# Neighbourhood attention block: sums of the output weights made in memory by accumulating transfers, another order of the last step's products, and the bias laid out in memory

## The chip, the core and the metric

The kernel runs on one core of a Trainium2 chip. The metric is device microseconds of one execution; the kernel before takes 899.82 us, the median of 3 runs (899.55 to 900.76). Engines are called as in the profile: PE multiplies matrices, PEld loads its weights, DVE and ACT work element by element, POOL and SP issue transfers (POOL also computes a few small values), and each engine works off its instructions in order. A profile of one execution shows every instruction with its times.

## The reference

One layer of an encoder over 512 tokens (an 8 x 64 grid) of width 2048, all in float32. The weights are two matrices, 2048 x 8192 in and 2048 x 2048 out.

```python
h = rms_norm(x, norm_pre)
q, k, v, z = jnp.split(h @ na_w_in, 4, axis=-1)          # 16 heads of 128
# each token attends to 8 rows x 16 columns of keys around its own column
s = einsum('bqhd,bxqyhd->bhqxy', q_r, k_nb) * scale + rpb[:, dr, dc]
o = einsum('bhqxy,bxqyhd->bqhd', softmax(s), v_nb)
y = (o * silu(z)) @ na_w_out
out = x + rms_norm(y, norm_post)
```

## The kernel before

Work goes in ten steps. Steps 0 to 7 multiply the input by the columns of the in-weights that two heads need (512 columns a step, the q, k, v and z of one pair of heads); steps 8 and 9 multiply the gated attention by the out-weights, 1024 columns in each. Steps 0 and 8 are plain products (32 k-steps, each 12 matmuls). Steps 1 to 7 and 9 use Strassen's scheme in Winograd's form: seven passes of eight k-steps, 6 matmuls in a k-step, over sums of blocks of the input (A11, S1, A12, N2, A22, N4, N3, made once) and sums of blocks of the weights (made as they come). Every float32 operand is split into `hi` (rounded, by ACT) and `lo` (the rest, by DVE), and a product is three matmuls: hi x hi, the input's lo x hi, hi x lo. A k-step is called m, and `base(step)` is a step's first; `k` below is the k-step inside a pass.

`prep(m)` makes `hi` and `lo` of the weights of k-step m, two k-steps (`AHEAD`) before the products; three buffers of each exist. The weights come from two places. `T[k]`, eight buffers, holds the running sum of weight blocks: pass 0 takes it as loaded, passes 1, 3 and 4 add a block to it on DVE (L234), pass 5 adds another for pass 6 (L249). `raw`, four buffers (`NRAW`), takes the blocks that are added or used as they are; SP issues a raw's load as soon as the buffer is free, that is when DVE has used the raw of four k-steps of that kind before.

In the last step (step 9, `LAST`) the passes run in the order `LATE`, pass 2 last, so that its result, which only the first two row blocks need, comes in two halves. `chain(p)` names the accumulator of a pass: X for 0 and 2, Y for 1, 3 and 5, Z for 4 and 6. `combine` reads the accumulators after a pass and keeps `c["12"]`, `c["21"]`, `c["22"]`. The 512 rows of the result are four blocks t; blocks 0 and 1 come from pass 5 (columns n = 3) and pass 2 (n = 2), blocks 2 and 3 from pass 6. `finish(n, t, ...)` squares a piece on ACT and scales it by `gpost` on DVE; when all four pieces of a block have their squares, POOL computes `rcy`, and `final(t)` adds each piece to the residual `xres` (four updates on DVE) and stores it. `load_res` loads the residuals on SP: in the last step, those of blocks 2 and 3 at one per k-step from pass 1 on.

Work beside the products (the attention of the heads, residuals, ends) is hung on k-steps by `at(m, f)`. What is issued through `sync`, `dve`, `act` (class `InOrder`) keeps the order in which it is written; all else may be moved by the scheduler, so the order on an engine is not the order of the code.

The relative bias of a head is loaded by `load_bias` (POOL's queue) as 128 overlapping rows `braw`, and `bias` adds the mask to a reversed view of it on DVE, three operations a head, into `bm`, which `add_bias` adds to the scores. A head's gated result goes to memory (`graw`, POOL's queue) and comes back in step 8. The squares of x for the first norm are loaded (`sq`) during step 0.

## Time and profile before

| | us |
|---|---|
| median of 3 runs | 899.82 |
| the profiled execution | 903.68 |
| its span | 901.9 |
| PE busy | 880.9 |
| DVE busy | 755.3 |
| ACT busy | 561.2 |
| POOL busy | 29.7 |
| span from the last matmul's end (889.34) | 12.6 |

The span is the time from the first to the last record of the profiled execution; the execution's own time is 1.8 us longer. A profile's times are compared with each other, and the medians with each other. In a timeline row stand start, length, engine, line, operation, output<-inputs, and in brackets how long the engine had been idle and what ended that. A row of the stretches gives for each engine its busy time and the number of its instructions.

### The profile page before, as it was taken

Reading aid. Unit: us, or ns where it says so; the run is one execution under the profiler, and the core shown is the slowest. Engines: PE = TensorE matmul, PEld = TensorE weight load, DVE = VectorE, ACT = ScalarE, POOL = GpSimd, SP = SyncE. Lnnn points to the kernel's source line nnn. Section 1 sums busy time; section 2 is a strip of 40 time slices with the busy share of each in tenths; the row PEclk is TensorE's granted clock in tenths of the full one; section 3 lists DMA queues with packets and bytes.
Section 4 is the critical chain, followed back from the end, with each engine's and each line's share of the span. In section 5 each row is a group of like instructions: output and inputs, shape, how many; then the busy total and the mean of one; then the engine's idle time right before and its main releaser. Section 6 shows DMA issues by size and latency. Waiting matters only on the chain. (4 is left out here: it accounts for less than half of the span.)

```text
span 901.9 us, 13169 instructions
## 1 busy us (share of the span) xinstructions
PE 880.9 (98%) x4184; PEld 731.3 (81%) x4184; DVE 755.3 (84%) x1415; ACT 561.2 (62%) x1089; POOL 29.7 (3%) x59
## 2 busy tenths in 40 slices
...
GB/s 256 237 258 131 105 138 210 217 130 162 219 214 111 190 227 192 95 218 210 176 112 219 210 176 110 239 200 149 137 278 205 157 93 119 158 122 254 245 179 186
DMA packets 85878, 163.32 MB, mean 181 GB/s; under 512 B 10017, under 2 KB 10017, under 8 KB 85809
## 3 DMA queue, kind: packets, MB, share of 16 engines
...
q8 instruction: 32, 0.52, 0.2%
q10 hardware_dynamic: 432, 0.53, 0.2%
...
## 5 line engine op out<-in xcount | busy, mean ns | idle before, releaser
L241 ACT CAST hi<-t 128x512 fp32r<-128x512 f32 x320 | 196.8, 618 | 137.3 <-DVE lo L242 31.1
L242 DVE TENSOR_TENSOR lo<-t,hi 128x512 fp32r<-128x512 f32 x320 | 218.1, 687 | 25.8 <-ACT hi L241 24.9
L242 DVE TENSOR_TENSOR lo<-raw,hi 128x512 fp32r<-128x512 f32 x184 | 125.8, 689 | 62.8 <-ACT hi L241 50.3
L241 ACT CAST hi<-raw 128x512 fp32r<-128x512 f32 x184 | 113.6, 620 | 98.9 <-PE u L279 18.7
L234 DVE TENSOR_TENSOR t<-t,raw 128x512 f32<-128x512 f32 x192 | 128.5, 688 | 13.0 <-DMA raw<-in_w 12.5
L279 PE MATMUL u<-hi,a 128*128 128x512 f32 x512 | 133.1, 397 | 3.4 <-ACT hi L241 2.1
L279 PEld LDWEIGHTS u<-hi,a 128*128 128x128 f32 x512 | 96.2, 191 | 24.3 <-ACT hi L241 2.6
L279 PE MATMUL u<-lo,a 128*128 128x512 f32 x256 | 70.8, 390 | 0.0
L279 PEld LDWEIGHTS u<-lo,a 128*128 128x128 f32 x256 | 48.2, 188 | 10.1
L249 DVE TENSOR_TENSOR t<-t,raw 128x512 f32<-128x512 f32 x64 | 42.8, 688 | 1.2 <-DMA raw<-in_w 1.1
L149 DVE TENSOR_TENSOR a<-x,a 128x256 fp32r<-128x256 f32 (+1 forms) x24 | 11.6, 512 | 19.5 <-ACT a L148 19.5
L450 DVE TENSOR_TENSOR bm<-braw,mask_sb 128x256 f32<-128x256 f32 x48 | 27.4, 601 | 0.0
L322 PE MATMUL u1Y<-hi,a 128*128 128x512 f32 x96 | 26.8, 396 | 0.0
L322 PE MATMUL u6Y<-hi,a 128*128 128x512 f32 x96 | 26.8, 396 | 0.0
L322 PE MATMUL u5Y<-hi,a 128*128 128x512 f32 x96 | 26.8, 396 | 0.0
L322 PE MATMUL u7Y<-hi,a 128*128 128x512 f32 x96 | 26.8, 396 | 0.0
L322 PE MATMUL u3Y<-hi,a 128*128 128x512 f32 x96 | 26.8, 396 | 0.0
L322 PE MATMUL u4Y<-hi,a 128*128 128x512 f32 x96 | 26.8, 396 | 0.0
L322 PE MATMUL u2Y<-hi,a 128*128 128x512 f32 x96 | 26.8, 396 | 0.0
L322 PE MATMUL u9Y<-hi,a 128*128 128x512 f32 x96 | 26.6, 392 | 0.0
L444 POOL DMA_DIRECT2D braw<-in_rpb x16 | 8.5, 534 | 437.9 <-DVE bm L450 253.5
L322 PEld LDWEIGHTS u9Y<-hi,a 128*128 128x128 f32 x96 | 17.9, 188 | 4.3 <-ACT s L341 0.4
(444 smaller groups left out, 1953.2 us busy)
## 6 DMA issues: line engine op xcount, KB each, us to landing
raw<-in_w SPq DMA_DIRECT2D x384, 256.0 KB, 3.0
t<-in_w SPq DMA_DIRECT2D x128, 256.0 KB, 3.0
x<-in_xT SPq DMA_DIRECT2D x16, 256.0 KB, 4.4
xres<-in_x SPq DMA_DIRECT2D x16, 256.0 KB, 6.2
graw<-zm POOLq DMA_DIRECT2D x14, 256.0 KB, 3.7
out<-xres SPq DMA_DIRECT2D x14, 256.0 KB, 3.2
...
braw<-in_rpb POOLq DMA_DIRECT2D x16, 184.0 KB, 3.6
```

Source lines behind the costliest of these rows:

```text
L149: (vector or nc.vector).tensor_tensor(lo, src, hi.bitcast(F32), ALU.subtract)
L234: nc.vector.tensor_tensor(T[k], T[k], src, ALU.add)
L241: nc.scalar.copy(hi, src)
L242: nc.vector.tensor_tensor(lo, src, hi.bitcast(F32), ALU.subtract)
L249: nc.vector.tensor_tensor(T[k], T[k], src, ALU.add)
L279: nc.tensor.matmul(U[n][j], l, r, start=k == 0 and i == 0, stop=k == KT - 1 and i == 2)
L322: nc.tensor.matmul(U[c][s], l, r, start=p in (0, 1, 4) and k == 0 and n == 0, stop=k == KH - 1 and n == 2, skip_group_check=True,)
L444: nc.gpsimd.dma_start(raw[:, 0 : 7 * TBL + 32], src)
L450: nc.vector.tensor_tensor(bm[:, i, :].rearrange("p (a b) -> p a b", b=8), rev, mask_sb[:, i, :].unsqueeze(2).to_broadcast([P, 32, 8]), ALU ...
```

## The change

Five things change.

1. Sums of the out-weights for the last step. Four sums of weight blocks, which passes 1, 3, 4 and 6 of the last step need, are made in memory (`wsum`): a transfer copies one block there, a second one adds another block to it while it is written (`accum_op=ALU.add`), each for two of the eight k. These are 16 copies and 16 accumulations, 512 KB each, written on k-steps 10 apart from step 1 on, on POOL's queue. In the last step `T[k]` is then loaded anew for every pass but the last, right after its old content was split, and DVE adds nothing; only pass 2 uses `raw`.
2. The last step's passes run in the order 0, 1, 3, 4, 6, 5, 2. The pieces of blocks 2 and 3 are finished from the k-steps of pass 5 on, and their four updates are hung two to a k-step. DVE's end work is no longer held in written order.
3. The weights of the last pass are split beside earlier passes, one in two k-steps, and loaded up to 24 k-steps ahead. The residuals of blocks 2, 3 and 1 are loaded over 28 k-steps, about one in 2.5, those of block 0 into `T` during pass 5.
4. The bias, with the mask in it, is laid out on the host as the 128 x 3 x 256 table of each head; `load_bias` loads it straight into `bm`, and the mask's load and the 48 additions go.
5. In step 0 the input is loaded four k-steps ahead, not three, and step 1's first loads of T keep their written place behind the loads of the squares.

```diff
-LATE = (0, 1, 3, 4, 5, 6, 2)
+LATE = (0, 1, 3, 4, 6, 5, 2)
...
     def load_t(step, q, k):
-        nc.sync.dma_start(T[k], w[step, q, k])
+        (sync if step == 1 and q == B11 else nc.sync).dma_start(T[k], w[step, q, k])
+    wsum = dp.tile([4, KH, P, L], F32, name="wsum")
+    LATE_W = {0: w[LAST, B11], 1: wsum[0], 3: wsum[1], 4: wsum[2], 5: w[LAST, B22], 6: wsum[3], 2: w[LAST, B21]}
+    SUMS = ((0, w[LAST, B11], B12), (1, wsum[0], B22), (2, wsum[1], B21), (3, w[LAST, B12], B22))
+    def sum_w(i, k, add):
+        o, src, q = SUMS[i]
+        if add:
+            pool.dma_start(wsum[o, k : k + 2], w[LAST, q, k : k + 2], accum_op=ALU.add, max_dma_last_dim=8192)
+        else:
+            pool.dma_start(wsum[o, k : k + 2], src[k : k + 2], max_dma_last_dim=8192)
...
     def is_raw(m):
         step, p, _ = where(m)
-        return step in PLAIN or p not in (0, 6)
+        return step in PLAIN or (p == 2 if step == LAST else p not in (0, 6))
...
-        e = max(m - 6 if m < N - KH else 0, seq[i - NRAW] if i >= NRAW else 0)
+        e = max(m - (6 if m < N - KH else 24), seq[i - NRAW] if i >= NRAW else 0)
...
-        if not plain and p in (1, 3, 4):
+        if step < NSTEP and not plain and p in (1, 3, 4):
...
-        if plain:
+        if step == LAST:
+            i = LATE.index(p)
+            if i + 2 < NPASS:
+                nc.sync.dma_start(T[k], LATE_W[LATE[i + 1]][k])
+        elif plain:
...
-                finish(2, 2 + s, c["21"][:, s, :])
-                finish(3, 2 + s, c["22"][:, s, :])
...
     def load_bias(h):
-        raw = sp.tile([P, L], F32, tag="braw", name=f"braw{h}")
-        src = bass.AP(rpb.tensor, rpb.offset + h * 15 * TBL, [[1, 16], [TBL, 8], [1, 7 * TBL + 32]])
-        nc.gpsimd.dma_start(raw[:, 0 : 7 * TBL + 32], src)
-        bm_of[h] = (raw, sp.tile([P, 3, 256], F32, tag="bm", name=f"bm{h}"))
+        bm_of[h] = sp.tile([P, 3, 256], F32, tag="bm", name=f"bm{h}")
+        nc.gpsimd.dma_start(bm_of[h], rpb[h])
...
-    def final(t):
+    def final(t, qs=range(4)):
...
-            dve.scalar_tensor_tensor(r, yg[q, t], rcy[:, col], r, ALU.mult, ALU.add)
+            nc.vector.scalar_tensor_tensor(r, yg[q, t], rcy[:, col], r, ALU.mult, ALU.add)
...
-            if q % 2 == 0:
-                xres["c", q] = ag.tile([P, 2, L], F32, tag=f"a{q // 2}_1", name=f"xres{t}{q}")
-            xres[t, q] = xres["c", q - q % 2][:, q % 2, :]
+            xres[t, q] = T[q]
...
-    for k in range(KH):
-        t, q = divmod(k, 4)
-        at(base(LAST) + KH + k, load_res, 2 + t, q)
-        at(base(LAST) + (5 * KH + 2 * q + 1 if t == 0 else 2 * KH + 2 * q), load_res, t, q)
-    for s in range(2):
-        at(base(LAST) + 6 * KH + 1 + s, final, 2 + s)
+    for i, (t, q) in enumerate((t, q) for t in (2, 3, 1) for q in range(4)):
+        at(base(LAST) + KH + 5 * i // 2, load_res, t, q)
+    for q in range(4):
+        at(base(LAST) + 5 * KH + q, load_res, 0, q)
+    for i in range(4):
+        for j in range(KH):
+            at(base(1) + 10 * (KH * i + j), sum_w, i, j % 4 * 2, j // 4)
+    for s in range(2):
+        for n, key in ((2, "21"), (3, "22")):
+            at(base(LAST) + 5 * KH + 1 + 2 * s, lambda n=n, key=key, s=s: finish(n, 2 + s, C[LAST][key][:, s, :]))
+        for q in range(4):
+            at(base(LAST) + 5 * KH + 5 + 2 * s + q // 2, final, 2 + s, (q,))
...
-        if N - 2 * KH <= m + AHEAD < N - KH:
-            prep(m + AHEAD + KH)
-        if 0 <= m and m + 3 < KT:
-            load_x(m + 3)
+        if m >= N - 3 * KH + 4 and m % 2 == 0 and m < N - KH + 4:
+            prep(N - KH + (m - (N - 3 * KH + 4)) // 2)
+        if 0 <= m and m + 4 < KT:
+            load_x(m + 4)
```

The order on the engines shows what the scheduler makes of it, at three places. First POOL's queue from the start of the program, before (`mask_sb` and `braw` are the bias's loads, `rc` the first norm's factor, `graw` a head's store; in brackets what a row waits for):

```order
L628 DMA mask_sb<-in_mask 128x96
L444 DMA braw_946<-in_rpb 128x1x368
L444 DMA braw_1240<-in_rpb 128x1x368 [waits DMASW1_49,DVE_49]
L188 TENSOR_TENSOR rc<-ms,mhalf 128x4 [waits DVE_49,Pool_49]
L444 DMA braw_1812<-in_rpb 128x1x368 [waits DMASW2_49,DVE_49]
L549 DMA graw<-zm_1076 128x512 [waits DVE_49]
```

and now:

```order
L456 DMA bm_945<-in_rpb 128x768 [waits DVE_49,PE_49]
L64 DMA wsum<-in_w 64x2048
L199 TENSOR_TENSOR rc<-ms,mhalf 128x4 [waits DVE_49,Pool_49]
L64 DMA wsum<-in_w 64x2048
L456 DMA bm_1237<-in_rpb 128x768 [waits DMASW0_49,DVE_49]
L64 DMA wsum<-in_w 64x2048
L550 DMA graw<-zm_1072 128x512 [waits DVE_49]
L64 DMA wsum<-in_w 64x2048
L64 DMA wsum<-in_w 64x2048 [waits DMASW1_49]
L456 DMA bm_1808<-in_rpb 128x768 [waits DMASW3_49,DVE_49]
L550 DMA graw<-zm_1478 128x512 [waits DVE_49]
L64 DMA wsum<-in_w 64x2048 [waits DMASW2_49]
```

The first copy stands behind head 0's table (which waits for PE, since `bm` shares its buffer with the ones of PE's warm-up) and has no wait of its own; the later ones stand behind loads and stores that wait for DVE, and go out in groups behind these.

Second SP's queue in pass 1 of the last step, before (`raw` weight blocks, `xres` residuals):

```order
L64 DMA xres_8617<-in_x 128x1x512
L223 DMA raw_8624<-in_w 128x512
L64 DMA xres_8632<-in_x 128x1x512
L223 DMA raw_8639<-in_w 128x512
L64 DMA xres_8647<-in_x 128x1x512
L223 DMA raw_8654<-in_w 128x512
L64 DMA xres_8662<-in_x 128x1x512
L223 DMA raw_8669<-in_w 128x512
```

and now:

```order
L257 DMA t_142<-wsum 128x512
L64 DMA xres_8766<-in_x 128x1x512
L257 DMA t_143<-wsum 128x512
L64 DMA xres_8796<-in_x 128x1x512
L257 DMA t_144<-wsum 128x512
L64 DMA xres_8578<-in_x 128x1x512
L257 DMA t_145<-wsum 128x512
L257 DMA t_146<-wsum 128x512
L64 DMA xres_8602<-in_x 128x1x512
L257 DMA t_147<-wsum 128x512
L257 DMA t_148<-wsum 128x512
L257 DMA t_149<-wsum 128x512
```

The weight blocks come as sums into the eight buffers T, one per k-step, and the residuals stand farther apart.

Third DVE at the end of the program, before (`xres` rows are updates, the names after the arrow tell the block: y_3 and the pieces s_9, e of block 3, y_0 of block 0, y_1 of block 1; `c` is the scaled piece of the last pass):

```order
L64 SCALAR_TENSOR_TENSOR xres_8707<-s_9_8722,rcy,xres_8707 128x512
L64 SCALAR_TENSOR_TENSOR xres_8725<-e_8841,rcy,xres_8725 128x512 [waits DVE_49]
L64 TENSOR_TENSOR c_9_9170<-u9X_8509,gpost_8072 128x512 [waits Activation_49]
L64 TENSOR_SCALAR msy<-part,ms_152 128x1
L64 SCALAR_TENSOR_TENSOR xres_9105<-y_0_8118,rcy,xres_9105 128x512 [waits DMAHW3_49,Pool_49]
L64 SCALAR_TENSOR_TENSOR xres_9105<-y_0_8480,rcy,xres_9105 128x512 [waits DMAHW4_49]
L64 SCALAR_TENSOR_TENSOR xres_9156<-c_9_9170,rcy,xres_9156 128x512 [waits DMAHW5_49,DVE_49]
L64 SCALAR_TENSOR_TENSOR xres_9156<-s_9_8599,rcy,xres_9156 128x512 [waits DMAHW6_49]
L64 TENSOR_TENSOR c_9_9170<-u9X_8510,gpost_8072 128x512 [waits Activation_49]
```

and now, farther back, where blocks 2 and 3 are finished:

```order
L253 TENSOR_TENSOR lo_9025<-t_147,hi_9024 128x512 [waits DMAHW7_49,PE_49,Activation_49]
L659 TENSOR_TENSOR s_9_8661<-s_9_8661,gpost_8039 128x512
L661 TENSOR_REDUCE ms_152<-part 128x1
L659 TENSOR_TENSOR e_8762<-e_8762,gpost_8039 128x512
L662 TENSOR_SCALAR ms_152<-ms_152 128x1 [waits DVE_49]
L253 TENSOR_TENSOR lo_9046<-t_148,hi_9045 128x512 [waits DMAHW1_49,PE_49,Activation_49]
L664 TENSOR_SCALAR msy<-part,ms_152 128x1 [waits DVE_49]
L253 TENSOR_TENSOR lo_9058<-t_149,hi_9057 128x512 [waits DMAHW2_49,PE_49,Activation_49]
L671 SCALAR_TENSOR_TENSOR xres_8578<-y_2_8097,rcy,xres_8578 128x512 [waits Pool_49]
L671 SCALAR_TENSOR_TENSOR xres_8602<-y_2_8461,rcy,xres_8602 128x512
```

The scaling and the updates of blocks 2 and 3 stand among the `lo` operations of pass 5 instead of behind the whole pass 6; the last rows of the program are the two `c` with their four updates each, as before.

More of the change, by code (lines that the diff above doesn't have):

```diff
@@ L67, in na_block @@
 @with_exitstack
-def na_block(ctx: ExitStack, tc: tile.TileContext, xT, x, gpre, gpost, w, rpb, mask, out):
+def na_block(ctx: ExitStack, tc: tile.TileContext, xT, x, gpre, gpost, w, rpb, out):
     nc = tc.nc
-    sync, dve, act = (InOrder(tc, e) for e in (nc.sync, nc.vector, nc.scalar))
+    sync, dve, act, pool = (InOrder(tc, e) for e in (nc.sync, nc.vector, nc.scalar, nc.gpsimd))
     PSUM = bass.MemoryType.PSUM
@@ L99, in na_block @@
     nc.gpsimd.memset(mhalf, -0.5)
-    mask_sb = cp.tile([P, 3, 32], F32, name="mask_sb")
     edge = {}
@@ L441, in load_bias @@
     def load_bias(h):
-        raw = sp.tile([P, L], F32, tag="braw", name=f"braw{h}")
-        src = bass.AP(rpb.tensor, rpb.offset + h * 15 * TBL, [[1, 16], [TBL, 8], [1, 7 * TBL + 32]])
-        nc.gpsimd.dma_start(raw[:, 0 : 7 * TBL + 32], src)
-        bm_of[h] = (raw, sp.tile([P, 3, 256], F32, tag="bm", name=f"bm{h}"))
-    def bias(h, i):
-        raw, bm = bm_of[h]
-        rev = bass.AP(raw.tensor, raw.offset + 7 * TBL + 31, [raw.ap[0], [-1, 32], [-TBL, 8]])
-        nc.vector.tensor_tensor(
-            bm[:, i, :].rearrange("p (a b) -> p a b", b=8),
-            rev,
-            mask_sb[:, i, :].unsqueeze(2).to_broadcast([P, 32, 8]),
-            ALU.add,
-        )
+        bm_of[h] = sp.tile([P, 3, 256], F32, tag="bm", name=f"bm{h}")
+        nc.gpsimd.dma_start(bm_of[h], rpb[h])
     WIN = {0: (0, 64), 1: (64, 256), 2: (192, 0), 3: (256, 192)}
@@ L482, in add_bias @@
                 in0=s_of[h, a][:, base + lo : base + hi],
-                in1=bm_of[h][1][:, (0, 1, 1, 2)[i], lo:hi],
+                in1=bm_of[h][:, (0, 1, 1, 2)[i], lo:hi],
                 op0=ALU.add,
@@ L602, in na_block @@
         at(when(h, 0) - (4 if late else 11), load_bias, h)
-        for i in range(3):
-            at(when(h, i) if late else when(h, 0) - 7 + i, bias, h, i)
     for pr in range(NSTEP):
@@ L627, in na_block @@
         at(12 + 2 * i, lambda i=i: pending.pop(i)())
-    at(8, lambda: nc.gpsimd.dma_start(mask_sb, mask))
     at(28, rstd)
@@ L665, in finish @@
         if i == 3:
-            dve.tensor_scalar(msy[:, col], part[:, t, 3:4], 1.0 / D, ms3[:, col], ALU.mult, ALU.add)
+            nc.vector.tensor_scalar(msy[:, col], part[:, t, 3:4], 1.0 / D, ms3[:, col], ALU.mult, ALU.add)
             nc.gpsimd.tensor_tensor(rcy[:, col], msy[:, col], mhalf[:, 0:1], ALU.pow)
-    def final(t):
+    def final(t, qs=range(4)):
         col = slice(t, t + 1)
-        for q in range(4):
+        for q in qs:
             r = xres[t, q]
-            dve.scalar_tensor_tensor(r, yg[q, t], rcy[:, col], r, ALU.mult, ALU.add)
+            nc.vector.scalar_tensor_tensor(r, yg[q, t], rcy[:, col], r, ALU.mult, ALU.add)
             eng = nc.scalar if t == 1 and q % 2 else nc.sync
@@ L713, in na_block, with _bias @@
             f()
-def _mask():
-    m = np.full((P, 3, GRID_W // 2), NEG, np.float32)
+def _bias(rpb):
+    flat = np.pad(rpb[:, ::-1, ::-1], ((0, 0), (0, 0), (8, TBL - 39))).reshape(HEADS, -1)
+    c, r, a, b = np.ogrid[0:16, 0:ROWS, 0:32, 0:ROWS]
+    rel = flat[:, c + TBL * r + 7 * TBL + 31 - a - TBL * b].reshape(HEADS, P, 256)
+    tab = np.full((HEADS, P, 3, 256), NEG, np.float32)
     for typ, i in ((0, 0), (1, 1), (2, 3)):
@@ L754 @@
         "w": w,
-        "rpb": rpb,
-        "mask": _mask(),
+        "rpb": _bias(np.asarray(na_rpb)[0]),
     }
```

19 lines of the change are left out of this document (10 added, 9 removed).

## The prediction

> **What bounds the kernel now.** I read the page's span and busy times first, then the busy time by stretches of 20 us, then what the matmul engine waited for, and last the timeline at the three places that these point to.
>
> ```profile
> span 901.9 us, 13169 instructions
> PE 880.9 (98%) x4184; PEld 731.3 (81%) x4184; DVE 755.3 (84%) x1415; ACT 561.2 (62%) x1089; POOL 29.7 (3%) x59
> ```
>
> PE is the bound: only 21 us of the span are without a matmul. The change takes no product away, so at most those 21 us, and the time in which PE was busy but slow, can be won. The stretches (columns: PE, PEld, DVE, ACT, POOL busy us with counts, clock, DMA share, GB/s) say where that is:
>
> ```profile
> 20.00:40.00 20.00, 20.00 (x90) 16.55 (x89) 9.21 (x16) 12.91 (x25) 0.00 (x0) 1.00 0.82 228
> 40.00:60.00 20.00, 17.87 (x72) 14.34 (x71) 10.32 (x18) 11.14 (x21) 0.00 (x0) 0.91 0.97 274
> ...
> 180.00:200.00 20.00, 20.00 (x99) 16.68 (x98) 17.85 (x33) 15.01 (x27) 0.00 (x0) 1.00 0.49 142
> ...
> 300.00:320.00 20.00, 20.00 (x105) 16.80 (x104) 17.88 (x30) 11.27 (x20) 0.55 (x1) 1.00 0.81 236
> ...
> 820.00:840.00 20.00, 17.24 (x70) 12.17 (x69) 13.58 (x22) 7.80 (x13) 0.00 (x0) 1.00 1.03 268
> 840.00:860.00 20.00, 20.00 (x90) 16.56 (x89) 19.34 (x32) 9.33 (x15) 0.00 (x0) 1.00 0.71 227
> 860.00:880.00 20.00, 19.25 (x85) 15.44 (x84) 17.76 (x34) 12.61 (x26) 0.00 (x0) 1.00 0.60 170
> ```
>
> An undisturbed stretch of wide products has 90 matmuls. 40:60 is short of 18, 820:840 of 20, 860:880 of 5. In the stretches between, PE is full while the DMA share swings from 0.49 to 0.81: nothing is to be won there, only to be lost.
>
> ```profile
> PE u9Y L322 <- DVE lo L242: 2.8, 5, 1.2
> ```
>
> PE's longest waits in total are those of the last step, for DVE's `lo`, itself behind loads; next comes one at 47 us, shown below.
>
> **The tail: -3.3 us.**
>
> ```profile
> 888.64 0.75 DVE L64 SCALAR_TENSOR_TENSOR xres<-e,rcy,xres 128x512 f32<-128x512 f32 x1
> 888.95 0.39 PE L322 MATMUL u9X<-a 128*128 128x512 f32 x1
> 889.30 0.68 DVE L64 TENSOR_TENSOR c<-u9X,gpost 128x512 f32<-128x512 f32 x1
> ...
> 889.92 0.19 ACT L660 ACTIVATION_READ_ACCUMULATOR ysq<-u9X 128x1 f32 x1
> 890.18 0.54 POOL L667 TENSOR_TENSOR rcy<-msy,mhalf 128x1 f32<-128x1 f32 x1 [5.04 <-DVE msy L64]
> ...
> 893.41 0.68 DVE L64 TENSOR_TENSOR c<-u9X,gpost 128x512 f32<-128x512 f32 x1
> 894.01 0.20 DVE L64 TENSOR_SCALAR msy<-part,ms 128x1 f32<-128x1 f32 x1
> ...
> 896.87 0.75 DVE L64 SCALAR_TENSOR_TENSOR xres<-s,rcy,xres 128x512 f32<-128x512 f32 x1
> ```
>
> The last matmul ends at 889.34, 12.56 us before the span does. DVE is still at the row blocks t = 2 and 3 until 889.3, so block 0, whose sums were done half a pass earlier, begins only then, and block 1 at 893.41 although its squares were ready at 890.11. From there to the end are 8.49 us (scale, `rcy`, four updates, stores). With pass 6 ahead of pass 5, blocks 2 and 3 are worked off during pass 5 and the first half of pass 2. In the new order DVE has, between the end of pass 6 and block 0's `c`, 18 wide TENSOR_TENSORs, 8 updates and some ten small ones. By the step from 893.41 to 894.01 a wide one takes 0.60; an update takes at most 0.75; the small ones about 0.1 each: 10.8 + 6.0 + 1.0 = 17.8 us at most, and it can begin 0.6 before pass 6 ends, whose first half closes three products early: done at 17.2. Block 0 then needs 0.60 + 0.2 + 0.65 + 4 x 0.7 = 4.2: done at 21.4. PE meanwhile has 68 matmuls to block 0's half and 24 to block 1's, 92 x 0.2275 = 20.9, and block 1's squares are read 0.8 later, at 21.7. DVE is there in time, by a margin of 0.3 at the dearest prices. Block 1's `c` then starts at 890.13 of the old scale: gain 3.28. Bounds: 3.9, if `c` needs no squares and only `msy` waits for them (894.01 against 890.11), and 2.3, if DVE, whose `lo` operations go at PE's pace, runs 1.3 over.
>
> **The last step: -5.0 us.**
>
> ```profile
> 815.92 0.55 SPq L64 DMA_DIRECT2D xres<-in_x  x1
> 816.56 0.54 SPq L223 DMA_DIRECT2D raw<-in_w  x1
> ...
> 834.17 1.36 DVE L234 TENSOR_TENSOR t<-t,raw 128x512 f32<-128x512 f32 x2 [0.87 <-DMA raw<-in_w]
> ...
> 836.19 0.74 PE L322 MATMUL u9Y<-lo,a 128*128 128x512 f32 x2 [1.16 <-DVE lo L242]
> ```
>
> One residual load goes out per k-step beside one weight load, 2 x 262 KB per 6 x 0.2275 = 1.365 us, 384 GB/s wanted where the stretch moves 268 at share 1.03. `raw` has only four buffers, so its loads are late, then the add, then `lo`, then PE. In 860:880 the second cause is DVE and ACT, which prepare the last pass beside pass 6. Together 25 matmuls, 25 x 20/90 = 5.6 us. After the change there is no add in this step: 24 L234 and 8 L249 operations go, which are off the path wherever PE was full. Each weight block goes into T[k] eight k-steps (10.9 us) ahead instead of four, 12 residual loads are spread over 28 k-steps, and the last pass is prepared from pass 3 on. Still wanted: 1 + 12/28 loads per k-step, 274 GB/s, hardly more than what was moved; the surplus over 28 k-steps is 38.2 x 6/274 = 0.8 us, which the longer lead swallows. New is that pass 6 accumulates into the tiles that DVE (L353) has just to read after pass 4; ahead of PE's first product there stand 4 products of the last pass, 0.91 us, against two DVE operations of 0.60, the first of which can start three products (0.68) before pass 4 ends. For both I leave 0.6 lost. Bounds: all 5.6 won, or 2.5.
>
> **The early stall: -1.6 us.**
>
> ```profile
> 8.00:12.00 4.00, 3.51 (x16) 2.60 (x15) 1.98 (x5) 3.01 (x8) 0.00 (x0) 1.00 0.59 194
> ...
> 48.00:52.00 4.00, 4.00 (x12) 3.14 (x13) 2.32 (x4) 3.87 (x8) 0.00 (x0) 0.60 0.71 215
> ```
> ```profile
> 40.26 0.43 SPq L140 DMA_DIRECT2D x<-in_xT  x1
> ...
> 42.73 1.98 PE L279 MATMUL u<-hi,a 128*128 128x512 f32 x8
> 44.55 1.07 PE L279 MATMUL u<-lo,a 128*128 128x512 f32 x4
> 46.47 0.72 ACT L159 ACTIVATE x<-x,gcol 128x512 f32<-128x512 f32 x1 [1.94 <-DMA x<-in_xT]
> 47.09 0.60 ACT L241 CAST hi<-raw 128x512 fp32r<-128x512 f32 x1
> ...
> 47.75 3.69 PE L279 MATMUL u<-hi,a 128*128 128x512 f32 x8 [2.13 <-ACT hi L241]
> ...
> 51.27 1.09 PE L279 MATMUL u<-lo,a 128*128 128x512 f32 x4
> ```
>
> Eight matmuls take 1.82 us (42.73 to 44.55), 0.2275 each. The four `lo` end their turn at 45.46, PE idles 2.29, and the next eight take 3.52, 1.70 too much, at a mean clock of 0.60. Loss 3.99. The cause is the last `x`, issued at 40.26 and landed 6.2 us later, with ACT's `hi` queued behind its scaling. The Trainium skill ("TensorE: Matmul & The Clock Gate", Part 1: The HAM clock gate) says that the array's clock halves after an idle window of about 3.4 us; the trace agrees on the half, but an idle time of 2.29 us was enough. By the page a stall of this length would cost 1.7 us less.
>
> The change sends x[9], x[10] and x[12] further ahead and moves the eight loads of T behind the squares' loads. Against it:
>
> ```profile
> braw<-in_rpb POOLq DMA_DIRECT2D x16, 184.0 KB, 3.6
> ...
> mask_sb<-in_mask POOLq DMA_DIRECT2D x1, 48.0 KB, 4.3
> ```
> ```profile
> 1.05 5.49 PE L97 MATMUL warm<-ones 128*128 128x128 f32 x24 [1.05 <-DVE ones L94]
> ...
> 16.95 0.53 POOL L444 DMA_DIRECT2D braw<-in_rpb  x1 [14.16 <-DVE bm L450]
> ```
>
> The first sum's copy stands in POOL's queue right behind head 0's bias, which waits for PE's warm-up to leave its buffer (6.54), and goes out at some 7 us, and the bias is 393 KB where mask and `braw` were 236 KB: 0.68 MB more, 2.5 us at 274 GB/s; `braw` of head 1 (188 KB) goes out later, which leaves 1.8. About 1.6 of it fits where the share was 0.59 (0.41 x 4). Bounds: all 3.99 won, or 1.8 lost more. I take 1.6, a little above the middle.
>
> **The sums on the way: +2.5 us.** No row shows a transfer from memory to memory; the nearest are
>
> ```profile
> raw<-in_w SPq DMA_DIRECT2D x384, 256.0 KB, 3.0
> graw<-zm POOLq DMA_DIRECT2D x14, 256.0 KB, 3.7
> ```
> ```profile
> 174.72 0.55 POOL L549 DMA_DIRECT2D graw<-zm  x1 [0.69 <-DVE zm L543]
> ...
> 312.74 0.55 POOL L549 DMA_DIRECT2D graw<-zm  x1 [18.97 <-DVE zm L543]
> ```
>
> 16 copies and 16 accumulations of 524 KB. A copy at 268 GB/s is 1.96 us of all engines; an accumulation reads twice, I take twice that, 3.9 (from nothing, if hidden, to three passes, 5.9). POOL's queue does not let them out evenly: those queued behind a `graw` store go together. Behind the store of a pair's second head (174.72) two or three go out where the share is near 0.49, which hides them. Behind the first head's (the row at 312.74) two go out at share 0.81. With the store (1 us) they are 8.8 us of DMA time; between two queues I take half each, so 17.6 us, in which SP's loads fall behind by 17.6 x 0.31 = 5.5 us. The slack: a raw is issued four k-steps (5.46) ahead and lands in 3.0, leaving 2.5; preparing two k-steps ahead adds 2.73, less three operations of about 0.7: 3.1 in all. So 2.4 us lost in each of two such bursts, and 0.8 in one of three copies: 5.6. At one pass per accumulation none is lost. I take 2.5. The rest of the bias:
>
> ```profile
> L450 DVE TENSOR_TENSOR bm<-braw,mask_sb 128x256 f32<-128x256 f32 x48 | 27.4, 601 | 0.0
> ```
>
> 27.4 us leave DVE, which PE waits for in none of these stretches, and 16 loads grow by 0.2 MB each: at nothing, the raws' slack covers 0.8 us.
>
> **Sum.** -3.3 - 5.0 - 1.6 + 2.5 = -7.4 us. The profiled execution took 903.68, so 896.3 there; it lies 3.86 above the median of 899.82, and I carry the difference over: 892.4.
>
> **Rivals.**
> - *All cover holds.* Sums hidden, early stall gone: 3.9 + 5.6 + 4.0 = 13.5, 886.3. For it: shares well under 1 from 60 to 800 us. Against: the burst arithmetic. 0.13.
> - *The early stall grows.* The first copy delays the last x by its full 1.8: -3.3 - 5.0 + 1.8 + 2.5, 895.8. 0.10.
> - *The last step is not mended.* Wanted 274 against moved 268: T's loads come late in place of `raw`, the 5.6 stay lost: 897.4. Against: twice the lead, no adds. 0.12.
> - *Slower: accumulations starve SP.* At four passes (7.8 us) the two dear bursts are 16.6 of DMA time each, 33 us long, lag 10.3, loss 7.2 each; with the smaller ones and two halved clocks some 20 us, less 9.9 won: 910. It decides from about 6 us per accumulation, where the two bursts lose 9.9 together. For it: no row prices one. 0.13. The Trainium skill ("DMA: Bandwidth & Descriptors", Queues, rings and completion order) has each DMA engine take turns between queues packet by packet, under which SP keeps its turn and this rival would be milder; no run here shows it yet.
>
> That leaves 0.52 for the forecast. About 0.2% (1.8 us) is what a measurement here can tell from no change. Faster 0.80, same 0.07, slower 0.13. The range for 8 in 10: from the first rival's end, 886.3, up to 899.5, which keeps most of what ends above 897 and leaves out the starved case and the far end of the bounds (902.4).
>
> **What would show it.** Right: block 1's `c` under 1 us behind the last matmul and 9.3 us before the end; 90 matmuls in every stretch of the last step; `hi` at 47 us not behind an x. Wrong: PE waiting for `lo` behind `raw` after 226, 312, 399 or 487 us; accumulations landing after more than 10 us; clock under 1 there; t<-wsum named as what DVE or ACT waits for in the last step; a growing wait for x before 50 us.

## The result, and the profile after

| | us |
|---|---|
| the changed kernel, median of 4 runs | 1063.53 (1058.30 to 1064.23) |
| the kernel before, beside it | 900.28 |
| ratio, with its 95% interval | 1.1802 (1.1763 to 1.1840) |
| the changed kernel's profiled execution, its span | 1063.53, 1061.8 |

The change makes the kernel 18% slower. The prediction, 892.4 us with 0.80 for faster, was off by 171 us.

The page of the changed kernel: the span, the engines' busy time, and PE's busy share in 40 slices.

```profile
span 1061.8 us, 13188 instructions
PE 926.9 (87%) x4184; PEld 762.0 (72%) x4184; DVE 729.1 (69%) x1335; ACT 564.4 (53%) x1089; POOL 52.1 (5%) x90
...
PE   9998989985998499957995799759994799999996
```

PE was idle 21 us before, now 135. The same 4184 matmuls were also busy 46 us longer (926.9 against 880.9), at a lower clock. The loss is no general slowness: it comes in dips, the last six of them evenly spaced. The stretches of 20 us around one of them (columns as in the prediction):

```profile
320.00:340.00 20.00, 20.00 (x90) 16.57 (x89) 15.45 (x25) 9.92 (x17) 0.00 (x0) 1.00 0.73 222
340.00:360.00 20.00, 7.87 (x33) 6.21 (x32) 10.91 (x27) 6.49 (x17) 0.56 (x1) 0.62 0.46 150
360.00:380.00 20.00, 12.70 (x67) 10.26 (x66) 11.17 (x27) 12.30 (x29) 5.54 (x8) 0.78 0.59 139
380.00:400.00 20.00, 20.00 (x93) 16.66 (x92) 14.93 (x24) 9.52 (x16) 0.00 (x0) 1.00 0.72 203
```

320:340 holds 90 matmuls, wide products and nothing else; before, 300:320 held 105, since a head's small matmuls stood among them. Then PE nearly stops, and the clock falls to 0.62. The transfer engines are half idle there (share 0.46), so it is not a lack of bandwidth that holds PE. PE's longest wait in total, and the timeline at that place:

```profile
PE pt L515 <- ACT edge L509: 93.9, 11, 11.7
```
```profile
341.63 0.39 PE L337 MATMUL u3Y<-lo,a 128*128 128x512 f32 x1
...
349.32 0.69 DVE L264 TENSOR_TENSOR t<-t,raw 128x512 f32<-128x512 f32 x1 [0.52 <-DMA raw<-in_w]
349.93 0.35 DVE L481 CUSTOM_DVE_ANT_0 edge<-s,bm 128x192 f32<-128x192 f32 x1
...
351.03 0.46 ACT L500 ACTIVATE edge<-edge,nm 128x192 f32<-128x192 f32 x1 [8.58 <-DVE nm L493]
...
351.62 0.56 POOL L456 DMA_DIRECT2D bm<-in_rpb  x1 [87.63 <-DVE nm L493]
...
353.40 0.48 PE L515 MATMUL pt<-ident,edge 128*128 128x128 f32 x1 [11.37 <-ACT edge L509]
```

PE has done pass 3 of step 3 and comes to head 3's transposes. DVE first makes operands for passes still to come (up to 349.32), then adds head 3's bias (349.93); the exponentials (351.03) and the normalization follow, and PE starts at 353.40, 11.37 us later. The bias table was not late: POOL had waited 87.63 us for these additions, to load the next head's. Between 345 and 349.32 DVE waits 2.8 us for loads, 0.52 of it shown here; the rest of the wait is the order in which the instructions stand. PE's rows there, in the changed kernel (numbered in the order of the program):

```
1343 L337 MATMUL u3Y1_2985<-lo175_3344,a7_3_141 128x512
1344 L515 MATMUL pt3_0_2633<-ident_81,edge0_103 128x128
...
1362 L538 MATMUL o3_2707<-pt3_1h_2680,vl1_1_1938 128x256
1363 L416 MATMUL tk4_2892<-ident_81,c11_2_2296 128x2x64
...
1383 L468 MATMUL s4_1_2992<-k4h_2907,q4l_2927 128x256
1384 L515 MATMUL pt4_0_3154<-ident_81,edge0_103 128x128
```

Before, the same transposes of head 3 stood behind k-step 129, inside a pass of step 2, with products between each stage; now they stand behind k-step 175, and head 4's whole attention follows without one product in between. The k-step behind which each head's first transposes stand:

| head | 1 | 2 | 3 | 4 | 5 | 6 | 7 | 8 | 11 | 12 | 13 |
|---|---|---|---|---|---|---|---|---|---|---|---|
| before | 73 | 106 | 129 | 162 | 185 | 218 | 241 | 274 | 353 | 386 | 409 |
| changed | 102 | 119 | 175 | 175 | 231 | 231 | 287 | 287 | 399 | 399 | 409 |

From head 3 on, two heads share a place (9 and 10 likewise). The chain that ended last shows what a step then costs, and POOL's timeline of before, set beside the row at 312.74 in the prediction, what it cost (the same store one step later):

```profile
380.72 9.77 PE u3Z L337 x43
...
494.96 9.77 PE u4Z L337 x43
...
609.09 9.77 PE u5Z L337 x43
...
725.00 9.77 PE u6Z L337 x43
```
```profile
399.51 0.55 POOL L549 DMA_DIRECT2D graw<-zm  x1 [18.93 <-DVE zm L543]
```

A step takes 114.2 us (494.96 - 380.72) in place of 86.8 (399.51 - 312.74). Over six steps, from the first `u1Z` (pass 4 of step 1, at 156.1 us) to the first `u7Z` (at 834.7), it is 678.6 us, before 522.3 (150.7 to 673.0). These 156 us are nearly all of the 160 by which the span grew.

### The profile page after: what moved, and what is told of

Its sections match the earlier page's. It is cut to its first block, busy times and chain, and to the rows that moved or that the text cites. A ratio compares the mean times of both kernels' runs of the same rounds, so it can differ in the third digit from the quotient of the medians.

```text
span 1061.8 us, 13188 instructions
## 1 busy us (share of the span) xinstructions
PE 926.9 (87%) x4184; PEld 762.0 (72%) x4184; DVE 729.1 (69%) x1335; ACT 564.4 (53%) x1089; POOL 52.1 (5%) x90
## 3 DMA queue, kind: packets, MB, share of 16 engines
q0 software_dynamic: 6080, 30.41, 10.4%
## 4 chain that ended last, share of the span: by engine, by line
PE 64%; DVE 9%; DMA 8%; ACT 6%; issue 3%; SPq 0%; DVEq 0%; POOLq 0%; POOL 0%; ACTq 0%
PE u L294 8%; DMA raw<-in_w 7%; PE o L538 3%; PE u9Y L337 3%; DVE lo L253 3%; PE u2Y L337 3%; PE u3Y L337 2%; DVE t L245 2%; PE u1Y L337 2%; PE u6Y L337 2%; PE u5Y L337 2%; PE u4Y L337 2%; PE u6Z L337 2%; PE u4Z L337 2%; PE u3Z L337 2%
## 5 line engine op out<-in xcount | busy, mean ns | idle before, releaser
L252 ACT CAST hi<-t 128x512 fp32r<-128x512 f32 x328 | 202.3, 620 | 195.5 <-DVE lo L253 65.4
L253 DVE TENSOR_TENSOR lo<-t,hi 128x512 fp32r<-128x512 f32 x328 | 224.6, 689 | 81.0 <-ACT hi L252 71.9
L253 DVE TENSOR_TENSOR lo<-raw,hi 128x512 fp32r<-128x512 f32 x176 | 120.7, 689 | 70.4 <-ACT hi L252 52.5
L245 DVE TENSOR_TENSOR t<-t,raw 128x512 f32<-128x512 f32 x168 | 113.8, 688 | 19.1 <-DMA raw<-in_w 18.5
L515 PE MATMUL pt<-ident,edge 128*128 128x128 f32 x64 | 21.5, 394 | 93.9 <-ACT edge L509 93.9
L515 PEld LDWEIGHTS pt<-ident,edge 128*128 128x128 f32 x64 | 10.4, 185 | 100.1 <-ACT edge L509 99.5
L264 DVE TENSOR_TENSOR t<-t,raw 128x512 f32<-128x512 f32 x56 | 38.7, 691 | 26.9 <-DMA t<-in_w 17.1
L500 ACT ACTIVATE edge<-edge,nm 128x192 f32<-128x192 f32 x32 | 14.3, 448 | 63.1 <-DVE nm L493 63.1
L456 POOL DMA_DIRECT2D bm<-in_rpb x16 | 9.3, 579 | 627.2 <-DVE nm L493 553.5
L429 DVE TENSOR_TENSOR pt_0l<-pt,pt_0h 128x512 fp32r<-128x512 f32 x16 | 11.1, 691 | 28.3 <-ACT pt_0h L428 28.3
L544 DVE SCALAR_TENSOR_TENSOR zm<-o,zm 128x512 f32<-128x512 f32 x16 | 11.1, 691 | 27.9 <-PE o L538 27.9
L337 PE MATMUL u2Y<-hi,a 128*128 128x512 f32 x96 | 27.4, 401 | 0.0
```

The source lines that it names most:

```text
L245: nc.vector.tensor_tensor(T[k], T[k], src, ALU.add)
L252: nc.scalar.copy(hi, src)
L253: nc.vector.tensor_tensor(lo, src, hi.bitcast(F32), ALU.subtract)
L264: nc.vector.tensor_tensor(T[k], T[k], src, ALU.add)
L337: nc.tensor.matmul(U[c][s], l, r, start=p in (0, 1, 4) and k == 0 and n == 0, stop=k == KH - 1 and n == 2, skip_group_check=True,)
L429: nc.vector.tensor_tensor(lo, t, hi.bitcast(F32), ALU.subtract)
```

## The experiments

Three theories stood at the start. ORDER: the scheduler put the heads in the wrong place, because of the sums in POOL's queue. TRAFFIC: the sums' transfers slow the weight loads. BIAS TABLE: the larger table arrives late. A run is called by its short name, e1 to e17.

**The sums left out (e1).** The 32 `sum_w` go, and `T[k]` takes single blocks.

```diff
-            at(base(1) + 10 * (KH * i + j), sum_w, i, j % 4 * 2, j // 4)
+            pass
```

> The changed kernel with the 32 sum transfers left out; in the last step T[k] is loaded from single weight blocks in place of the sums, so the products of passes 1, 3, 4 and 6 there are of other operands, with the same number and size of loads. Theory ORDER (the sums stand in POOL's queue ahead of the bias loads, the scheduler therefore writes heads 1 to 12 a pass or more later, two heads one behind the other, and PE stands in their chains): the heads' rows come back to their old places, 888 to 893 us. Theory TRAFFIC (the sums' 32 transfers slow the loads of weights): also about 890. Theory BIAS TABLE (384 KB a head into a single buffer come late by themselves): the table is still there, over 1000 us.

891.87 us, ratio 0.9887 (0.9860 to 0.9915). All heads are back in their places, with the table in use: BIAS TABLE falls. The rest of the change is worth 1.1%, nearly what the prediction gave it.

**Copies (e3), a quarter of the bytes (e7), PE's order alone (e4).** Three edits of the changed kernel: no accumulation; transfers of 128 KB; PE's instructions (not ACT's and DVE's) held in written order.

```diff
-            pool.dma_start(wsum[o, k : k + 2], w[LAST, q, k : k + 2], accum_op=ALU.add, max_dma_last_dim=8192)
+            pool.dma_start(wsum[o, k : k + 2], w[LAST, q, k : k + 2], max_dma_last_dim=8192)
...
+            pool.dma_start(wsum[o, k : k + 1, 0:64], w[LAST, q, k : k + 1, 0:64], accum_op=ALU.add, max_dma_last_dim=8192)
...
-            nc.tensor.transpose(dst, src, ident)
+            pe.transpose(dst, src, ident)
```

> The changed kernel with the 16 accumulating transfers turned into plain copies of the same 512 KB, so the sums hold one block only. The order on PE is the same as in the changed kernel. ORDER: 1060 us, within 5. TRAFFIC: the reads of the old content go, 16 x 512 KB of them, a third of the sums' bytes: at least a quarter of the 163 us back, under 1025 us. BIAS TABLE: 1060 us.

> The changed kernel with each of the 32 transfers cut to a quarter of its bytes (64 rows of one block in place of two blocks of 128), and T[k] loaded from single weight blocks in the last step, so the products of passes 1, 3, 4 and 6 there are of other operands. The scheduler still writes heads 2 to 12 late, in pairs, as in the changed kernel; only head 1 keeps its place. ORDER (the late heads cost some 134 us by themselves, 1063.5 less 929.4, and the bursts of transfers some 37, 929.4 less 891.9): 1005 to 1045 us. If the late heads cost little without the traffic: under 950 us.

> The changed kernel with PE's instructions kept in written order, which is that of before; POOL's queue stays as changed, and on ACT the exponentials of heads 1 to 12 stay right ahead of the transposes that need them. ORDER: the two heads of a pair come apart and run inside the passes again; what stays is one chain from add_bias to the transposes for each of 12 heads, 3.5 us (from DVE at 349.9 to PE at 353.4 in the changed kernel) plus up to as much for a halved clock: 920 to 985 us. TRAFFIC and BIAS TABLE: 1060 us, since PE then waits for the same transfers in other places.

Copies: 1059.97, as ORDER has it. A quarter of the bytes: 1054.29, above the range I expected and 162 us above no sums, so the late heads cost nearly all of the loss whatever is moved. PE's order alone: 1105.27, a miss, and worse than the changed kernel. Its waits:

```profile
PE pt L64 <- ACT edge L509: 156.0, 24, 18.4
```

The bias additions on DVE and the exponentials on ACT still stood right ahead of the transposes, so PE now met the chain at 24 places in place of 11. The order is one over three engines; putting back one of them helps nothing.

**The sums alone in POOL's queue (e2).** The bias loads, the heads' stores and their loads go out from ACT.

```diff
-        nc.gpsimd.dma_start(bm_of[h], rpb[h])
+        nc.scalar.dma_start(bm_of[h], rpb[h])
...
-            nc.gpsimd.dma_start(graw[h], z_of[h])
+            nc.scalar.dma_start(graw[h], z_of[h])
...
-        nc.gpsimd.dma_start(X[h], graw[h])
+        nc.scalar.dma_start(X[h], graw[h])
```

> The changed kernel with the bias loads, the stores of the gated heads and their loads in step 8 issued by ACT, so that the sums have POOL's queue to themselves. All transfers are as in the changed kernel. ORDER: 890 to 897 us (the forecast of 892.4 is for this order). TRAFFIC: nothing is taken away, over 1000 us. BIAS TABLE: the loads wait for the same buffer, over 1000 us.

959.58 us: all heads are back, and yet 68 us are lost against no sums. Neither theory had that. The stretches show a second cause:

```profile
100.00:120.00 20.00, 15.71 (x72) 12.47 (x71) 12.07 (x29) 10.84 (x24) 5.69 (x9) 0.91 1.02 291
120.00:140.00 20.00, 15.22 (x57) 11.34 (x56) 5.27 (x9) 6.02 (x13) 5.67 (x9) 0.82 1.03 303
140.00:160.00 20.00, 13.12 (x38) 9.42 (x37) 5.70 (x9) 4.06 (x7) 3.15 (x4) 0.59 1.01 298
```

With no store to wait for, POOL lets the 32 sums out one close behind the other from 80.77 to 148 us, and until 160 us the transfer engines are full. That costs 30 of the 68 us: the first product of the last step starts at 832.2 us, in e1 at 802.2. The other 39 are lost in the last step, which takes 125.9 us to the end of the span in place of 86.8: there the scheduler now puts loads of T far from where they are due, and ACT waits 26.3 us for them. A stretch of it:

```profile
880.00:900.00 20.00, 15.81 (x51) 11.83 (x50) 6.01 (x10) 4.45 (x8) 0.00 (x0) 0.74 0.43 133
```

**The same transfers, written otherwise (e5, e6).** The scheduler sees 256 rows of 512 in place of 2 x 128 x 512. What is issued is 64 rows of 8 KB in both.

```diff
-            pool.dma_start(wsum[o, k : k + 2], src[k : k + 2], max_dma_last_dim=8192)
+            pool.dma_start(wsum[o, k : k + 2].rearrange("k p l -> (k p) l"), src[k : k + 2].rearrange("k p l -> (k p) l"), max_dma_last_dim=8192)
```

In e6 the rows are of 2 KB as well:

```diff
+            pool.dma_start(wsum[o, k : k + 2].rearrange("k p l -> p k l"), src[k : k + 2].rearrange("k p l -> p k l"))
```

> The changed kernel with the sums' transfers written as 256 rows of 512 in place of 2 x 128 x 512. What is issued is the same: 64 rows of 8 KB, the same 32 transfers, on POOL's queue, at the same places among the bias loads and stores but for one; only the scheduler then leaves heads 1 to 12 where they were before, on PE, ACT and DVE. ORDER: 889 to 897 us (the forecast of 892.4 is for this order; without the sums it was 891.87), and PE waits for `edge` before a transpose for under 3 us in all, against 93.9. TRAFFIC and BIAS TABLE: nothing is taken away, 1060 us.

> As e5_rows256, but the sums are moved in rows of 2 KB (128 x 2 x 512), four times as many. Order as in e5_rows256. ORDER: within 3 us of e5_rows256. If the sums cost the weight loads time by their rows and not by their bytes (a form of TRAFFIC): over 3 us slower than e5_rows256.

929.39 us, ratio 1.0331 (1.0298 to 1.0365), and 921.23, ratio 1.0224 (1.0196 to 1.0253) with rows of 2 KB. Neither came where it was expected: e5 lies 32 us above ORDER's range, and smaller rows are faster by 8 us, not equal or slower. The wait for `edge` is gone, and 134 us with it: what had moved the heads was the scheduler's plan, which hangs on how a transfer is written (what it reckons for the one form and the other stays open). But 37 us more than without the sums remain, all of them ahead of the last step (its first product starts at 841.8 us, in e1 at 802.2). One of the places, by the stretches, the timeline and the transfer queues (packets, MB, share of the engines' time; then the loads with their median us to landing) of the first of the two:

```profile
300.00:320.00 20.00, 20.00 (x100) 16.76 (x99) 14.67 (x23) 10.75 (x19) 0.28 (x1) 1.00 0.76 205
320.00:340.00 20.00, 13.44 (x59) 11.01 (x58) 12.00 (x23) 7.86 (x14) 1.94 (x3) 0.83 0.74 201
```
```profile
319.72 0.57 POOL L550 DMA_DIRECT2D graw<-zm  x1 [21.30 <-DVE zm L544]
320.28 1.66 POOL L64 DMA_DIRECT2D wsum<-in_w  x2
...
332.63 1.39 DVE L245 TENSOR_TENSOR t<-t,raw 128x512 f32<-128x512 f32 x2 [6.69 <-DMA raw<-in_w]
333.95 0.68 DVE L423 SCALAR_TENSOR_TENSOR q5l<-tq,q5h 128x512 fp32r<-128x512 f32 x1
...
334.68 0.58 PE L468 MATMUL s<-k5h,q5l 128*128 128x256 f32 x1 [6.56 <-DVE q5l L423]
```
```profile
q0 software_dynamic: 125, 0.76, 74.0%
q1 hardware_dynamic: 214, 0.41, 20.4%
...
raw<-in_w SPq DMA_DIRECT2D x3, 256.0 KB, 9.8
```

The queues' rows are of 322 to 328 us. Two sums leave behind a head's store (320.28), and their queue takes 74% of the engines' time, SP's 20%. Behind eight other stores their queue has 58 to 87% of six us, SP's 10 to 39%. Raws land after 9.8 us in place of 3.0. DVE waits 6.69 us at an addition, with head 5's `q5l` queued behind it, and PE 6.56 us for that, at a mean clock of 0.83. With rows of 2 KB, at the same place (321 to 327 us), SP keeps more, and raws land after 8.4 us:

```profile
q0 software_dynamic: 342, 0.68, 63.8%
q1 hardware_dynamic: 401, 0.73, 41.7%
```

A new theory, BURST: it is the sums that leave together that cost.

**Sums held to their own k-step (e10_paced2k, e10_paced8k, e11).** Each sum now waits for the products of the k-step it is written at (`done`: the matmuls written so far).

```diff
+        tc.add_manual_dep(d.ins, done[-1], mybir.DependencyInfo(mybir.DependencyClass.Sync, mybir.DependencyReason.DATA), reason="pace")
```

> e6_rows2k with every sum made to wait for the products of its own k-step, so that they leave POOL 10 k-steps apart and not in twos and threes behind a store. BURST (the sums of a burst take the transfer engines from SP for 10 us, raws land after 10 to 12 us in place of 2.9, DVE's add waits with q's split behind it, and PE for that): one sum at a time at half the engines is 7.5 us for a copy and 11 for an accumulation, SP lags at most 11 x (0.8 - 0.5) = 3.3 us, about its slack: 890 to 900 us. TRAFFIC by bytes alone, whenever they are moved: 921 us as e6_rows2k, within 4.

> e5_rows256 (rows of 8 KB) with the same waits. In its bursts the sums' queue took 70 to 78% of the transfer engines' time and SP's 13 to 23%. BURST: with 78% an accumulation is 7.2 us and SP lags 7.2 x (0.8 - 0.2) = 4.3 us, 1.2 over its slack: 16 accumulations cost some 1 to 2 us each where SP is busy, 898 to 915 us, and slower than e10_paced2k by 5 us or more. If only the bursts counted and not the rows' size: within 3 us of e10_paced2k. TRAFFIC by bytes: 929 us, within 4.

> As e10_paced2k, but one block of 256 KB a transfer, 64 of them, 6 k-steps apart. BURST: SP lags 5.5 x 0.3 = 1.7 us at most, under its slack: 889 to 896 us, and not slower than e10_paced2k. If each transfer costs something by itself (issue, completion): slower than e10_paced2k by 2 us or more.

908.50 (ratio 1.0085, 1.0067 to 1.0104), 913.81 (1.0143, 1.0122 to 1.0165) and 910.75 (1.0118, 1.0100 to 1.0136). In either size of rows 42 to 43% of what the sums cost goes (15.6 of 37.5 us, 12.7 of 29.4). Rows of 2 KB do better than rows of 8 KB by 5.3 us, as expected; halving the transfers gains nothing (2.2 us slower, with intervals that just overlap, so whether a transfer costs something by itself stays open). The form with 8 KB came in its range, the other two missed theirs by 8 and 15 us: a sum by itself still costs where the loads are dense, 16.6 us in all in the best form.

**The sum made in SBUF (e12).** No `wsum`: in the last step the next block is added into `T[k]` by the load itself.

```diff
-                nc.sync.dma_start(T[k], LATE_W[LATE[i + 1]][k])
+                load_late(LATE[i + 1], k)
...
+            nc.gpsimd.dma_start(T[k], w[LAST, {1: B12, 3: B22, 4: B21, 6: B22}[p], k], accum_op=ALU.add)
```

> The changed kernel with no sums in memory: in the last step a transfer adds the next weight block straight into T[k] (accumulating, on POOL's queue, eight k-steps ahead, where the changed kernel loads a sum); pass 6 loads a block and adds a second one to it. The result is the reference's. 32 accumulating loads of 256 KB take the place of 32 transfers of 512 KB and 32 loads, and nothing of it runs beside steps 1 to 8. BURST and ORDER: what is left of both goes, as without the sums: 888 to 895 us, so faster than before. If an accumulating load lands later than its lead of 10.9 us: PE waits for `hi` behind t in the last step and the gain of the last step goes, 895 to 905 us.

902.83 us, ratio 1.0035 (1.0014 to 1.0057): no gain. Steps 1 to 8 run clean, and the last step loses it all. The rows of the loads and the stretches:

```profile
t<-in_w SPq DMA_DIRECT2D x136, 256.0 KB, 2.9
...
t<-in_w POOLq DMA_DIRECT2D x32, 256.0 KB, 8.8
```
```profile
820.00:840.00 20.00, 18.45 (x81) 14.76 (x80) 10.65 (x17) 11.07 (x20) 8.72 (x10) 1.00 1.12 216
840.00:860.00 20.00, 15.54 (x62) 12.38 (x61) 11.51 (x19) 6.57 (x11) 7.04 (x8) 0.91 1.09 288
```

An accumulating load lands after 8.8 us, a plain one of the same size after 2.9, and the engines are full in 820:860. The answer for loads that land later than their lead of 10.9 us came true, range and cause. On the chain that ended last stand one such load that took 11.32 us, with ACT's `hi` behind it, and two plain raws that took 7.88 and 10.73:

```profile
813.64 11.32 DMA t<-in_w
825.06 0.62 ACT hi L246
...
843.19 7.88 DMA raw<-in_w
...
853.94 10.73 DMA raw<-in_w
```

**The same transfers where the engines are idle (e15, and e16 two k-steps later).** As e10_paced2k, at other k-steps: the first eleven of each of steps 1 to 7, and step 8, where the transfers' share is low without the sums.

```diff
-            at(base(1) + 10 * (KH * i + j), sum_w, i, j % 4 * 2, j // 4)
+    slots = [base(s) + c for s in range(1, NSTEP) for c in (0, 5, 10)]
+    slots += [base(NSTEP) + 5 * c // 2 for c in range(32 - len(slots))]
...
+            at(slots[KH * i + j], sum_w, i, j % 4 * 2, j // 4)
```

> e10_paced2k with the 32 sums moved to the places where the transfers' share is low without them: k-steps 0, 5 and 10 of each of steps 1 to 7 (shares 0.15 to 0.55 there without the sums, against 0.6 to 0.85 in passes 1 to 5) and 11 in step 8 (share 0.4), each still waiting for its own k-step's products. Same bytes, same rows. PLACE (the 16 us that e10_paced2k still loses against no sums come from sums that run beside raws and T loads): 891 to 898 us, faster than before. BYTES (they cost wherever they run): 905 to 910 us.

> As e15_idle_places with the sums of steps 1 to 7 two k-steps later (2, 7 and 12). PLACE: the third then ends beside pass 1's raws (share 0.5 to 0.8): the same to 4 us slower than e15_idle_places. BYTES: the same, 905 to 910 us.

892.37 us, ratio 0.9896 (0.9879 to 0.9913), and 893.07, ratio 0.9905 (0.9885 to 0.9925): 1% faster than the kernel before, and 0.5 and 1.2 us above no sums at all, which the intervals do not tell apart. At these places the bytes cost next to nothing. The page of e15, and the stretches of its last step:

```profile
span 891.6 us, 13129 instructions
PE 877.3 (98%) x4184; PEld 729.5 (82%) x4184; DVE 714.6 (80%) x1335; ACT 559.5 (63%) x1089; POOL 61.0 (7%) x90
```
```profile
780.00:800.00 20.00, 20.00 (x90) 16.57 (x89) 15.73 (x31) 8.80 (x15) 2.27 (x2) 1.00 0.86 234
800.00:820.00 20.00, 20.00 (x90) 16.57 (x89) 12.23 (x20) 11.97 (x24) 0.00 (x0) 1.00 0.66 190
820.00:840.00 20.00, 20.00 (x88) 16.22 (x88) 11.67 (x18) 11.73 (x21) 0.00 (x0) 1.00 0.95 272
840.00:860.00 20.00, 19.59 (x86) 15.45 (x85) 15.09 (x25) 10.44 (x18) 0.00 (x0) 1.00 0.83 252
860.00:880.00 20.00, 20.00 (x90) 16.57 (x89) 19.25 (x41) 8.07 (x21) 3.00 (x3) 1.00 0.64 193
```

**The written shape put back (e17)** into e15, rows and places unchanged.

```diff
-            d = pool.dma_start(wsum[o, k : k + 2].rearrange("k p l -> p k l"), src[k : k + 2].rearrange("k p l -> p k l"))
+            d = pool.dma_start(wsum[o, k : k + 2], src[k : k + 2], max_dma_last_dim=2048)
```

> e15_idle_places with its transfers written again as 2 x 128 x 512, in rows of 2 KB as in e15: the same bytes in the same rows at the same waits. The scheduler then writes heads 1 to 13 late again, in pairs. ORDER (the late heads cost the same whether or not the transfers are well placed): 1045 to 1075 us. If the place of the sums had been the larger part after all: under 950 us.

1079.57 us, 5 above ORDER's range. One edit of how the transfer is written is worth 187 us. 151 of them lie between the first `u1Z` and the first `u7Z` (673.9 us, in e15 523.0); the rest, in steps 8 and 9, was not followed up.

**Step 0 undone (e8, e13) and the bias undone (e9, e14)**, on e5_rows256 and on e12_sum_into_sbuf.

```diff
-            load_x(m + 4)
+            load_x(m + 3)
```
```diff
-        bm_of[h] = sp.tile([P, 3, 256], F32, tag="bm", name=f"bm{h}")
-        nc.gpsimd.dma_start(bm_of[h], rpb[h])
+        raw = sp.tile([P, L], F32, tag="braw", name=f"braw{h}")
...
+            at(when(h, i) if late else when(h, 0) - 7 + i, bias, h, i)
```

> e5_rows256 with step 0 as before: x loaded three k-steps ahead, and step 1's first loads of T free to move. The prediction's term for this edit (-1.6 us, bounds -4.0 and +1.8): 1.6 us slower than e5_rows256, with PE waiting about 2.3 us behind the last x at 47 us as before. If the edit is worth all of the stall: 4 us slower. If the sums delay the last x so that the edit only breaks even: the same.

> e12_sum_into_sbuf with step 0 as before (x three k-steps ahead, step 1's loads of T free to move). No sum stands in POOL's queue here, so the edit is priced alone. The prediction's bounds for it: all of the early stall, 4.0 us slower than e12_sum_into_sbuf, or, with the 384 KB table still ahead of the last x, less.

> e5_rows256 with the bias as before: 188 KB a head loaded, and the mask added on DVE (48 operations, 27.4 us). The prediction puts this edit at nothing: within 1 us of e5_rows256. If DVE's 27.4 us stand on the path in some stretch: 2 us slower or more. If the 384 KB table costs the weight loads time: faster than e5_rows256 by 1 us or more.

> e12_sum_into_sbuf with the bias as before. With the sums in memory undoing it cost 6.6 us (935.96 against 929.39). If DVE's 27.4 us only hurt where DVE has just waited for a late raw (BURST): within 1 us of e12_sum_into_sbuf, as the prediction has it. If they stand on the path by themselves: 4 us or more slower.

Step 0 undone: 929.08 against 929.39, and 901.67 against 902.83; no gain from that edit in either. Bias undone: 935.96 (1.0388, 1.0365 to 1.0412) against 929.39 (1.0331, 1.0298 to 1.0365), intervals that just touch, and 905.27 against 902.83, intervals that overlap (1.0042 to 1.0088, 1.0014 to 1.0057); the 2.4 us lie between what the two answers expected. The stretch of the early stall, of e14 and then of e13:

```profile
40.00:60.00 20.00, 17.91 (x78) 14.16 (x77) 10.07 (x18) 12.75 (x23) 0.00 (x0) 1.00 0.81 214
```
```profile
40.00:60.00 20.00, 20.00 (x90) 16.48 (x89) 12.14 (x22) 13.39 (x24) 0.00 (x0) 1.00 1.01 279
```

Without the table 78 matmuls, with it and the old step 0 the full 90. One such stretch tells little, though: in the six runs whose sums start only after 90 us, which are written alike up to there, it holds 83 to 90, and in e8 it is full (89) after an earlier stall (73 matmuls in 0:20, 86 in e5). The start of step 1's first product takes step 0 as a whole:

| | on e12, us | on e5, us |
|---|---|---|
| both edits as changed | 93.0 | 95.8 |
| step 0 as before (e13, e8) | 93.4 | 96.2 |
| bias as before (e14, e9) | 97.7 | 102.5 |

In the kernel before it is 98.4. So it is the table that mends step 0, by 4.7 and 6.7 us, and the new order of the loads is worth 0.4, as far as one profile of each tells. What in the old bias holds step 0 up was not looked at. Behind step 0 DVE's 27.4 us cost nothing that these profiles show: from there to the end of the span e9 takes 829.2 us and e5 833.4, e14 806.5 and e12 807.6.

## Why the prediction was wrong

*What failed.* The step that failed is a term that the sum does not have. It rests on one sentence on what bounds the kernel: "In the stretches between, PE is full while the DMA share swings from 0.49 to 0.81: nothing is to be won there, only to be lost." The working that followed looked for losses in these stretches from transfers alone, and took PE's, ACT's and DVE's order in steps 1 to 7 as given, at no cost and without a reason. The edit did not touch it in the code, but the scheduler wrote it anew: heads 1 to 12 moved by 13 to 46 k-steps. That cost 134 us by e5 (1063.53 - 929.39) and 162 by e7, where nearly nothing was moved (1054.29 - 891.87). The order shown with the change was POOL's, SP's and DVE's at three places, and PE's in none of these steps. e5, e7 and e17 show the cause: the same transfers cost nothing of it when written otherwise, and nearly all of it with a quarter of the bytes. Why the scheduler orders the one form so and not the other stays open.

*The sums on the way, +2.5.* The mechanism was right (sums queued behind a `graw` store go out together, raws fall behind, DVE and then PE wait), the size was not: 37.5 us (929.39 - 891.87). A single sum was not priced too low. POOL's queue has 4.7% of e1's span of 889.0 us, 8.5% of e3's 1058.1 and 10.4% of the changed kernel's 1061.8; from these I estimate 1.5 us of all engines for a copy and 2.8 for an accumulation, where the term had 1.96 and 3.9. What was mis-sized is the share, "between two queues I take half each", where SP's queue had 20%, and the count, "two such bursts", where groups of two or three left behind ten stores. And the clock fell to 0.83 to 0.91 in five stretches, for which the term had nothing. The changed kernel hides most of this cost inside the larger one; it shows only when the heads are back.

*The rivals.* "Accumulations starve SP" has this mechanism and a price of 910, but its condition, about 6 us of all engines per accumulation, did not come true (2.8 by the estimate above). The 6.3 in the changed kernel's row is a time to landing, of 16 accumulations and 8 copies together:

```profile
wsum<-in_w POOLq DMA_DIRECT2D x24, 512.0 KB, 6.3
```

It is not what made 1063 us either. No rival had the order. The Trainium skill ("DMA: Bandwidth & Descriptors", Queues, rings and completion order) says that each transfer engine takes turns between queues packet by packet, and the prediction drew from it that SP keeps its turn and the rival would be milder. In 322:328 SP's queue moved 214 of the packets that the profile counts and the sums' queue 125; but these 125 took 74% of 6 us of 16 engines, 0.57 us each, and SP's 0.09. Whether single turns were kept no row shows, and a packet of the profile need not be one of the page; but turns, kept or not, were no equal share of the time.

*The tail, -3.3.* Right. Without the sums, the last matmul ends at 879.72 and the span at 889.0: 9.3 us in place of 12.56. The row that was to show it is there, 0.81 us behind that matmul:

```profile
880.53 0.69 DVE L659 TENSOR_TENSOR c<-u9X,gpost 128x512 f32<-128x512 f32 x1 [1.13 <-ACT ysq L658]
```

*The last step, -5.0.* Near. In e15's five stretches 6 of 450 matmuls are missing, 1.3 us at 20/90 each, where 0.6 was left: 4.3 won. From the first product of the last step to the end of the span it is 94.7 us before and 87.2 in e15: 7.5 won, where tail and last step together were given 8.3.

*The early stall, -1.6.* The row of the changed kernel:

```profile
40.00:60.00 20.00, 18.95 (x82) 15.01 (x81) 12.19 (x22) 13.48 (x26) 0.00 (x0) 1.00 0.81 199
```

82 matmuls of 72 before and 90 in full: 2.2 us. The last product of step 0 starts at 95.14 us, before at 98.22: 3.1 won, and step 1 starts 4.0 earlier in e15, where no copy goes out in step 0. Both lie within the bounds (up to 3.99), the second at their end. The cause given was wrong: loads of x sent further ahead won next to nothing, and the table, put among what speaks against it, is what helps.

*The rest of the bias at 0.* Right in the steps behind step 0, as far as the profiles of e9 and e14 show.

So the forecast of 892.4 holds for the edits without the reordering and the bursts, and not for the kernel as it was written. That e15's 892.37 meets it to the tenth is luck all the same. In the profiles of before and e15 the span falls by 10.3 us: 4.0 in step 0, 7.5 from the last step on, and 1.2 lost between, where 1.6, 8.3 and 2.5 were forecast, 7.4 in all; and the kernel before, beside e15, took 902.11 and not 899.82. Without the sums the terms give 9.9 us, and e1 is 9.8 under the 901.63 beside it.
